# Splitting the second mixer's weights, and making its memory keys and values, during the first layer's way down

## The chip, the cores and the metric

The kernel runs on one core of a Trainium2 chip. The core has five engines with their own instruction queues: TensorE (PE in the profile, with its weight loads as PEld) multiplies matrices, VectorE (DVE), ScalarE (ACT) and GpSimd (POOL) work on rows of 128 partitions, and SyncE (SP) issues the transfers between DRAM and the on-chip buffer SBUF. PE writes its products into PSUM. Each engine has its own queue of instructions and waits on semaphores for the others. The metric is the time of one execution in microseconds, the median of several runs.

## The reference

A hybrid encoder trunk over 512 tokens of width 1024, in float32. `DEPTH` is 2, so there are two layers: layer 0 has a banded window mixer (A), layer 1 a global mixer (B). Cut to what matters:

```python
mem_n = rms_norm(mem, mem_norm_g)                  # 256 memory rows, the same for both layers
for i in range(DEPTH):
    h = rms_norm(x, g_mix_pre[i])
    proj = h @ w_in[i]                             # q (12 heads of 64), k, v (3 heads), qm (4 heads)
    ...
    tok = mixer(q, k, v)
    mkv = mem_n @ w_mem_kv[i]                      # memory keys and values, 4 heads
    mo = memory_attention(qm, km, vm)
    o = concatenate([tok, mo]) @ w_o[i]
    x = x + rms_norm(o, g_mix_post[i])
    h = rms_norm(x, g_ffn_pre[i])
    gu = h @ w_gate_up[i]
    f = (silu(gu[..., :D_FF]) * gu[..., D_FF:]) @ w_down[i]
    x = x + rms_norm(f, g_ffn_post[i])
```

The memory keys and values of layer 1 depend on the memory and on a weight only, not on anything that layer 0 computes.

## The kernel before

**Products of split numbers.** The operands of PE are typed fp32r. Each float32 operand is split into a high part (`hi`, the number copied to fp32r) and a low part (`lo`, the rest), and `mm3` (L218 to L222) makes a product out of three matmuls: hi by hi, hi by lo, lo by hi. A weight comes from DRAM in units of 128 x 1024 (512 KB; units of `wkv` are 128 x 768, 384 KB). `unit` (L185) loads a unit into a buffer `raw` (three of them), then `split` (L224) writes `hi` and `lo` into a ring of four slots each in the pool `whl`. The high part is made on ACT (L230) or POOL (L228), the low part on DVE (L234) or POOL (L232); a table of constants, `PACE`, says which for each unit of the mixers. A slot is free again when the last matmul that reads it is done. Other weights take slots of the same ring: the gate and up weights of the feed-forward part (`pair`, L891) and the units of `wd`.

**A mixer** (`mixer`, L622) lays its pieces of work on a time axis by constants of `PACE` (`put`), sorts them, and writes them out in that order; this is PE's order. The other engines' orders, SP's among them, are set when the kernel is compiled. In layer 1 the pieces are, by position: the keys and values of four token tiles (`kv_pieces`, with four units of `wkv`), the first group of queries (`q_pieces`, two units of `wq` for each of four groups), the memory keys and values in four pieces of two (`mem_pieces`, four units of `wm`; the first two lie behind the keys, the last two among the first queries), then sixteen heads of scores (`score`, L498; `score_mem`), transposes of the probabilities (`turn`, L569) and values (`value`, L583), with the queries of the next groups between them; at the end the first part of the output product (`heads_out`, four units of `wo`). The keys pass through a normalisation and a rotary embedding (`rope_b`, L388) on ACT, DVE and POOL, a split, and transposes on PE (`keys`, L365: L370 and L375, copied by ACT to `ka` and by DVE to `kb`).

**The memory rows.** The normalised memory, split and transposed, lies in `mT` (2 MB). Layer 0 makes it and stores it to DRAM (`spill`, L650); layer 1 loads it back in four transfers (L438).

**The feed-forward part** (`ffn`, L857) works in three lots of hidden columns (8, 6 and 8 tiles of 128; `LOTS`). In each lot `body` makes the hidden columns and `down` (L792) multiplies them by `wd` ("the way down"): for each half of the output and each unit of two tiles, 24 matmuls of 512 columns. Lots 0 and 1 have eight and six such steps. The third lot's way down is in `ffn_out` (L817), where the norms of the next layer's input follow token tile by token tile. Four units of `wd` for its second half are held at once.

Of the kernel before, what the change touches and what calls it, by code (L numbers as in the profile page):

```python
# [15 lines left out]
P = 128  # L16
# [4 lines left out]
DEPTH = 2  # L21
# [151 lines left out]
class Trunk:  # L173
    def __init__(self, tc, a):
        self.tc, self.nc, self.a = tc, tc.nc, a

    def pool(self, stack, name, side="left", **kw):
# [6 lines left out]

    def unit(self, src, side=0, pool=None, parts=1, put=None, x=0, dst=None, key=None):  # L185

        nc, n = self.nc, src.shape[-1]

        def load():
# [143 lines left out]
    def mem_pieces(self, l, mk, put, x0, dx, lag, xw):  # L333
# [23 lines left out]
        for u in range(4):  # L357
            for m in range(2):
                put(x0[u] + m * dx[u] / 2, lambda u=u, m=m: prod(u, m))

    def again(self, k2):

        self.nc.gpsimd.tensor_scalar(k2[:, :, P:], k2[:, :, :HD].bitcast(F32), 1.0, 1.0, op0=OP.mult, op1=OP.mult)
# [49 lines left out]
    def kv_pieces(self, l):  # L413
# [3 lines left out]
        self.vs = self.core.tile([P, NT, NG, P], F32R, name="vs", tag="vs")  # L417
        w = self.wkv if l == 0 else [self.unit(self.a["wkv"][l, u], side=self.side(l, "kw", u)) for u in range(4)]

        def prod(t, st, u):  # L420
# [8 lines left out]
            if u == 3:  # L429
                kv = ps[:, :384].rearrange("p (z h d) -> p z h d", z=2, d=HD)  # L430
                r = self.rs[:, t:t + 1]
                self.split_scaled(self.vs[:, t, :, :HD], self.vs[:, t, :, HD:], kv[:, 1], r)
                kx = self.core.tile([P, 4, HD], F32, tag="qx", name="kx", bufs=3)
                ins = nc.scalar.activation(kx[:, :NG], kv[:, 0], AF.Copy, scale=r).ins  # L434
                if l:
                    with self.tc.issue_after(ins):
                        z, ks = t // 2, slice(t % 2 * 4, t % 2 * 4 + 4)
                        nc.sync.dma_start(self.mT[:, z, ks].bitcast(F32), self.spill[:, z, ks])  # L438
                self.rope(l, kx, t, NG, 1)
                st["k2"] = self.core.tile([P, 4, 3 * HD], F32R, tag="q2", name="k2", bufs=3)  # L440
                self.split(st["k2"][:, :NG, :HD], st["k2"][:, :NG, HD:P], kx[:, :NG])
                self.again(st["k2"][:, :NG])
# [8 lines left out]
    def q_pieces(self, l, c, qTs, put, x0, lead):  # L451
        nc = self.nc
        w = {}
        for z in range(2):
            self.unit(self.a["wq"][l, c, z], self.side(l, "qw", 2 * c + z), put=put, x=x0 - lead + z * lead / 3, dst=w,
                      key=z)

# [164 lines left out]
    def mixer(self, l, mkp, late, tokp):  # L622
# [19 lines left out]
        def keys():  # L642
            for m in range(2):
# [84 lines left out]
    def heads_out(self, l, put, xw, xs, x0, dx):  # L728
# [3 lines left out]
        for u in range(4):  # L732
            self.unit(self.a["wo"][l, 0, u], self.side(l, "owm", u), put=put, x=xw + u / 4, dst=self.wo, key=u)

# [82 lines left out]
    def ffn_out(self, get, w, fs, o, head, gpost, gpre, resid, dst, rs):  # L817
# [16 lines left out]
        for u in range(nu):  # L834
            wu = head["w"] if u == 0 else self.unit(w[0, fs[0] // 2 + u])
            for t in range(0 if u else 2, NT):
                self.down_prod(ps[t], get, fs, u, t, wu)
        for t in range(NT):
            join(ps[t], t, 0)
# [17 lines left out]
    def ffn(self, l, pools, forms, late, done):  # L857
# [152 lines left out]
        pools["forms"].close()  # L1010

        for c, (f0, f1) in enumerate(LOTS):
            fs = list(range(f0, f1))
# [6 lines left out]
            p1(gs[0])  # L1020
            p2(gs[0])
            prep_b(gs[0])
            prep_d(gs[0])
# [58 lines left out]
    def run(self):  # L1082
        tc, nc, a = self.tc, self.nc, self.a
        with ExitStack() as top:
# [5 lines left out]
            self.ps, self.nbank = self.psum(top, "ps"), 0  # L1090
            dram = top.enter_context(tc.tile_pool(name="dram", bufs=1, space=bass.MemoryType.DRAM))
            xs = [[dram.tile([P, D], F32, name=f"x{i}{t}", tag=f"x{i}{t}") for t in range(NT)] for i in range(3)]
# [17 lines left out]
            for l in range(DEPTH):  # L1110
# [4 lines left out]
                mkp = self.pool(core, f"mk{l}")  # L1115
                self.mT = tokp.tile([P, 2, KD, NMEM], F32R, tag="tok", name="mT", bufs=1)
                if l == 0:
                    late = self.start(mkp)
                norm.close()
                self.core = self.pool(core, f"core{l}")  # L1120
# [54 lines left out]
```

## Time and profile before

| | |
|---|---|
| median of 3 runs | 1162.95 us (1162.56 to 1165.04) |
| the profiled execution | 1161.5 us, of which the span from first to last instruction is 1159.7 us |
| mean granted clock of TensorE | 0.988 |
| first mixer and its output | about 30 to 220 us |
| feed-forward part of layer 0 | about 220 to 570 us |
| second mixer | about 570 to 767 us |
| DMA traffic | 124.06 MB, mean 107 GB/s |

The page gives busy times of the engines; the views of the trace give single instructions with start, duration and what ended the engine's idle time before them. A matmul's duration is its way through the array; matmuls follow each other faster than that, so the distance of their starts is what they cost. The clock column of a table of windows is the share of full speed that TensorE was granted.

### The profile page before, as it was taken

Reading aid. Unit: us, or ns where it says so; the run is one execution under the profiler, and the core shown is the slowest. Engines: PE = TensorE matmul, PEld = TensorE weight load, DVE = VectorE, ACT = ScalarE, POOL = GpSimd, SP = SyncE. Lnnn points to the kernel's source line nnn. Section 1 sums busy time; section 2 is a strip of 40 time slices with the busy share of each in tenths; the row PEclk is TensorE's granted clock in tenths of the full one; section 3 lists DMA queues with packets and bytes.
Section 4 is the critical chain, followed back from the end, with each engine's and each line's share of the span. In section 5 each row is a group of like instructions: output and inputs, shape, how many; then the busy total and the mean of one; then the engine's idle time right before and its main releaser. Section 6 shows DMA issues by size and latency. Waiting matters only on the chain.

```text
span 1159.7 us, 19436 instructions
## 1 busy us (share of the span) xinstructions
PE 1106.9 (95%) x7448; PEld 1016.6 (88%) x7448; DVE 840.9 (73%) x1432; ACT 644.7 (56%) x1308; POOL 264.6 (23%) x394
## 2 busy tenths in 40 slices
PE   5999989999999999999898999799999999999997
PEld 4989878899989989998788888577999899899985
DVE  5678884798637866885778998846997458658854
ACT  5568783665425534653436888845665246436531
POOL 6445573200000000000454764433000000000001
PEclk9999999999999999999999999999999999999999
DMA  7521124533422342225523110234234323413243
GB/s 269 189 74 37 37 74 134 189 114 109 154 65 73 110 145 73 97 87 191 174 93 106 37 37 2 69 116 150 68 115 140 107 73 110 142 41 110 92 163 109
DMA packets 34316, 124.06 MB, mean 107 GB/s; under 512 B 3872, under 2 KB 4000, under 8 KB 34096
## 3 DMA queue, kind: packets, MB, share of 16 engines
q1 hardware_dynamic: 33984, 122.24, 32.0%
q8 instruction: 58, 0.95, 0.3%
q0 software_dynamic: 240, 0.60, 0.2%
q14 instruction: 34, 0.28, 0.1%
HBM read 112.33 MB, written 10.49 MB: 106 GB/s over the span
## 4 chain that ended last, share of the span: by engine, by line
PE 78%; DVE 9%; ACT 5%; POOL 3%; issue 3%; DMA 1%; SPq 0%; POOLq 0%; DVEq 0%; ACTq 0%
PE ps L220 12%; PE ps L221 12%; PE ps L222 12%; PE ps L930 11%; PE ps L932 11%; PE ps L931 11%; PE tp L576 2%; PE o L591 1%; PE o L590 1%; PE s L511 1%; DVE tl L234 1%; PE s L512 1%; DMA raw<-in_wkv_dram 1%; ACT whi L230 1%; ACT p L528 1%
## 5 line engine op out<-in xcount | busy, mean ns | idle before, releaser
L230 ACT ACTIVATE whi<-raw 128x1024 fp32r<-128x1024 f32 (+2 forms) x177 | 150.6, 860 | 208.6 <-PE ps L222 104.2
L234 DVE TENSOR_TENSOR wlo<-raw,whi 128x1024 fp32r<-128x1024 f32 (+2 forms) x171 | 171.5, 1009 | 89.9 <-ACT whi L230 74.2
L930 PE MATMUL ps<-sf,whi 128*128 128x256 f32 x640 | 180.3, 282 | 0.1
L932 PE MATMUL ps<-sf,whi 128*128 128x256 f32 x640 | 180.2, 282 | 0.0
L931 PE MATMUL ps<-sf,wlo 128*128 128x256 f32 x640 | 179.8, 281 | 0.0
L254 POOL TENSOR_SCALAR e<-sso 128x1 f32<-128x1 f32 x8 | 3.4, 423 | 634.7 <-ACT junk L249 634.6
L220 PE MATMUL ps<-whi,f 128*128 128x512 f32 x352 | 137.3, 390 | 0.0
L222 PE MATMUL ps<-whi,f 128*128 128x512 f32 x352 | 137.0, 389 | 0.0
L221 PE MATMUL ps<-wlo,f 128*128 128x512 f32 x352 | 137.0, 389 | 0.0
L930 PE MATMUL ps<-a,whi 128*128 128x256 f32 x480 | 134.5, 280 | 0.0
L932 PE MATMUL ps<-a,whi 128*128 128x256 f32 x480 | 134.0, 279 | 0.0
L931 PE MATMUL ps<-a,wlo 128*128 128x256 f32 x480 | 133.9, 279 | 0.0
L930 PEld LDWEIGHTS ps<-sf,whi 128*128 128x128 f32 x640 | 121.2, 189 | 1.1 <-ACT p L936 0.6
L931 PEld LDWEIGHTS ps<-sf,wlo 128*128 128x128 f32 x640 | 120.9, 189 | 0.5
L932 PEld LDWEIGHTS ps<-sf,whi 128*128 128x128 f32 x640 | 121.1, 189 | 0.0
L220 PE MATMUL ps<-whi,hT 128*128 128x256 f32 (+1 forms) x320 | 101.6, 318 | 1.8 <-ACT kx L434 1.8
L221 PE MATMUL ps<-wlo,hT 128*128 128x256 f32 (+1 forms) x320 | 96.8, 303 | 4.6 <-DVE wlo L234 3.4
L222 PE MATMUL ps<-whi,hT 128*128 128x256 f32 (+1 forms) x320 | 96.4, 301 | 0.8 <-DVE hT L234 0.8
L566 POOL TENSOR_SCALAR p<-p,rd 128x256 f32<-128x256 f32 (+2 forms) x128 | 74.9, 603 | 76.2 <-DVE rd L563 23.0
L930 PEld LDWEIGHTS ps<-a,whi 128*128 128x128 f32 x480 | 90.3, 188 | 0.2
L931 PEld LDWEIGHTS ps<-a,wlo 128*128 128x128 f32 x480 | 90.2, 188 | 0.2
L932 PEld LDWEIGHTS ps<-a,whi 128*128 128x128 f32 x480 | 90.2, 188 | 0.0
(202 smaller groups left out, 2805.0 us busy)
## 6 DMA issues: line engine op xcount, KB each, us to landing
raw<-in_wgu_dram SPq DMA_DIRECT2D x48, 512.0 KB, 4.3
raw<-in_wd_dram SPq DMA_DIRECT2D x44, 512.0 KB, 4.3
rb<-in_wgu_dram SPq DMA_DIRECT2D x40, 512.0 KB, 3.6
raw<-in_wq_dram SPq DMA_DIRECT2D x16, 512.0 KB, 3.8
raw<-in_wo_dram SPq DMA_DIRECT2D x16, 512.0 KB, 3.5
xt<-x SPq DMA_DIRECT2D x12, 512.0 KB, 4.1
raw<-in_wm_dram SPq DMA_DIRECT2D x8, 512.0 KB, 4.0
x<-y SPq DMA_DIRECT2D x8, 512.0 KB, 2.9
```

What stands on the lines that cost most here:

```text
L220: mm(out, lh, rh, start=first, stop=False)
L221: mm(out, lh, rl, start=False, stop=False)
L222: mm(out, ll, rh, start=False, stop=last)
L230: nc.scalar.activation(hi, src, AF.Copy)
L234: nc.vector.tensor_sub(lo, src, hi.bitcast(F32))
L511: nc.tensor.matmul(s[:, :n], qi, hd["ka"]()[:, k0 * P:k1 * P], start=True, stop=False)
L512: nc.tensor.matmul(s[:, :n], qi, hd["kb"]()[:, k0 * P:k1 * P], start=False, stop=True)
L566: self.pooled = nc.gpsimd.tensor_scalar(hd["p"][z][:, :n], hd["p"][z][:, :n], rd[:, z:z + 1], 1.0, op0=OP.mult, op1=OP.mult)
L576: nc.tensor.transpose(tp[:, z], hd["p"][i][:, jj * P:(jj + 1) * P], self.ident)
L930: mm(out, wh[:, s], rh, start=start and k == 0, stop=False, skip_group_check=True)
L931: mm(out, wl[:, s], rh, start=False, stop=False, skip_group_check=True)
L932: mm(out, wh[:, s], rl, start=False, stop=k == 3, skip_group_check=True)
```

## The change

`ahead` splits a unit of layer 1 in layer 0 and stores both halves in DRAM; `unit` with the new argument `pair` loads such halves straight into two slots of the ring, without `raw` and without a split. Sixteen units go this way: four of `wkv`, eight of `wq`, four of `wo` (the first half of its columns). One is done after each step of `down` in layer 0 (8 in lot 0, 6 in lot 1) and two in `ffn_out`.

`mem_ahead` loads `mT` from DRAM into a pool of its own after lot 0's `down`, takes the four units of `wm`, makes layer 1's memory keys and values for both tiles of 128 rows (48 matmuls), and leaves the transposes of the keys and the stores to DRAM for the place behind the first two products of lot 1. The mixer of layer 1 loads the result in three transfers (512 KB each); its `mem_pieces` and its four loads of `mT` are gone.

```diff
+    def ahead(self, name, *at):
+        nc, src = self.nc, self.a[name][at]
+        pair = self.unit(src)
+        n = src.shape[-1]
+        self.pairs[(name,) + at] = [self.dram.tile([P, n], F32, name="pair", tag="_".join(map(str, (name, z) + at)))
+                                    for z in range(2)]
+        for z in range(2):
+            nc.sync.dma_start(self.pairs[(name,) + at][z], pair[z][:, :n].bitcast(F32))
...
+        if pair in self.pairs:
+            def fetch():
+                t = [self.whl.tile([P, 1024], F32R, tag=z, name=f"w{z}", bufs=4) for z in ("hi", "lo")]
+                for z in range(2):
+                    nc.sync.dma_start(t[z][:, :n].bitcast(F32), self.pairs[pair][z])
+                return t
+
+            if put is None:
+                return fetch()
+            put(x, lambda: dst.__setitem__(key, fetch()))
+            return
...
+    def mem_ahead(self, l, pool):
+        nc = self.nc
+        mT = pool.tile([P, 2, KD, NMEM], F32R, tag="mT", name="mT", bufs=1)
+        nc.sync.dma_start(mT.bitcast(F32), self.spill)
+        mk = {z: pool.tile([P, NMH, NMEM], F32R, name=f"km{z}", tag=f"km{z}", bufs=1) for z in "ab"}
+        mk["v"] = pool.tile([P, 2, NMH, P], F32R, name="vm", tag="vm", bufs=1)
+        w = [self.unit(self.a["wm"][l, u]) for u in range(4)]
+        out = []
+        for m in range(2):
+            ps = self.tagged("s")
+            for k in range(KD):
+                ms = (slice(None), k, slice(m * P, (m + 1) * P))
+                c = slice((k % 2) * 512, (k % 2) * 512 + 512)
+                self.mm3(ps, mT[:, 0][ms], mT[:, 1][ms], w[k // 2][0][:, c], w[k // 2][1][:, c], k == 0, k == KD - 1)
...
+            out.append(lambda m=m, k2=k2: self.keys(k2, mk["a"], mk["b"], m, 4))
+
+        def store():
+            for z, t in mk.items():
+                self.kept[z] = self.dram.tile(list(t.shape), F32, name="kept", tag=f"kept{z}")
+                nc.sync.dma_start(self.kept[z], t.bitcast(F32))
+
+        return out + [store]
...
-        w = self.wkv if l == 0 else [self.unit(self.a["wkv"][l, u], side=self.side(l, "kw", u)) for u in range(4)]
+        w = self.wkv if l == 0 else [self.unit(self.a["wkv"][l, u], pair=("wkv", l, u)) for u in range(4)]
...
-                ins = nc.scalar.activation(kx[:, :NG], kv[:, 0], AF.Copy, scale=r).ins
-                if l:
-                    with self.tc.issue_after(ins):
-                        z, ks = t // 2, slice(t % 2 * 4, t % 2 * 4 + 4)
-                        nc.sync.dma_start(self.mT[:, z, ks].bitcast(F32), self.spill[:, z, ks])
+                nc.scalar.activation(kx[:, :NG], kv[:, 0], AF.Copy, scale=r)
...
+            for z, t in mk.items() if l else ():
+                nc.sync.dma_start(t.bitcast(F32), self.kept[z])
...
-        self.mem_pieces(l, mk, put, xm, [pc["m0dur"], pc["m0dur"], pc["mdur"], pc["mdur"]], pc["mlag"], xw)
+        if l == 0:
+            self.mem_pieces(l, mk, put, xm, [pc["m0dur"], pc["m0dur"], pc["mdur"], pc["mdur"]], pc["mlag"], xw)
...
+                if self.todo:
+                    self.ahead(*self.todo.pop(0))
...
+            for z in later:
+                z()
+            mst.close()
+            later = []
...
+                if l < DEPTH - 1 and c == 0:
+                    later = self.mem_ahead(l + 1, self.pool(mst, "mem", side="right"))
...
+                    self.todo = ([("wkv", 1, u) for u in range(4)] + [("wq", 1, c, u) for c in range(4) for u in range(2)]
+                                 + [("wo", 1, 0, u) for u in range(4)])
```

The queries and the output product pass `pair=("wq", l, c, z)` and `pair=("wo", l, 0, u)` to `unit` in the same way. The constants of `PACE` are the same before and after.

More of the change, by code (lines that the diff above doesn't have):

```diff
@@ L455, in q_pieces @@
             self.unit(self.a["wq"][l, c, z], self.side(l, "qw", 2 * c + z), put=put, x=x0 - lead + z * lead / 3, dst=w,
-                      key=z)
+                      key=z, pair=("wq", l, c, z))
         def prod(t, st, u):
@@ L642, in keys @@
         def keys():
-            for m in range(2):
+            for m in range(0 if l else 2):
                 self.ready(("m", m))
@@ L732, in heads_out @@
         for u in range(4):
-            self.unit(self.a["wo"][l, 0, u], self.side(l, "owm", u), put=put, x=xw + u / 4, dst=self.wo, key=u)
+            self.unit(self.a["wo"][l, 0, u], self.side(l, "owm", u), put=put, x=xw + u / 4, dst=self.wo, key=u,
+                      pair=("wo", l, 0, u))
         def part(k):
@@ L837, in ffn_out @@
                 self.down_prod(ps[t], get, fs, u, t, wu)
+            if self.todo:
+                self.ahead(*self.todo.pop(0))
         for t in range(NT):
@@ L1010, in ffn @@
         pools["forms"].close()
+        later, mst = [], ExitStack()
         for c, (f0, f1) in enumerate(LOTS):
@@ L1090, in run @@
             self.ps, self.nbank = self.psum(top, "ps"), 0
-            dram = top.enter_context(tc.tile_pool(name="dram", bufs=1, space=bass.MemoryType.DRAM))
+            dram = self.dram = top.enter_context(tc.tile_pool(name="dram", bufs=1, space=bass.MemoryType.DRAM))
+            self.kept = {}
             xs = [[dram.tile([P, D], F32, name=f"x{i}{t}", tag=f"x{i}{t}") for t in range(NT)] for i in range(3)]
```

11 lines of the change are left out of this document (9 added, 2 removed).

## The prediction

> **What bounds the kernel now.** The head of the page comes first: which engine is full.
>
> ```profile
> span 1159.7 us, 19436 instructions
> PE 1106.9 (95%) x7448; PEld 1016.6 (88%) x7448; DVE 840.9 (73%) x1432; ACT 644.7 (56%) x1308; POOL 264.6 (23%) x394
> ```
>
> TensorE (PE) is idle for only 1159.7 - 1106.9 = 52.8 us, so a change that leaves the matmuls as they are can win some part of that, plus time in which the clock was low. The next view is the table of windows, ten microseconds each, over the second mixer (about 570 to 767 us); these are its rows with the most idle PE. Columns: busy time of PE, weight load, DVE, ACT, POOL, then granted clock, DMA share, GB/s.
>
> ```profile
> 570.00:580.00 10.00, 6.60 (x31) 6.06 (x30) 7.86 (x11) 3.93 (x9) 5.89 (x8) 0.77 0.73 222
> ...
> 600.00:610.00 10.00, 6.84 (x51) 6.19 (x49) 8.51 (x18) 3.88 (x10) 5.29 (x8) 0.98 0.52 175
> ...
> 650.00:660.00 10.00, 8.95 (x61) 7.56 (x60) 9.96 (x21) 9.05 (x21) 9.35 (x12) 1.00 0.17 53
> ...
> 690.00:700.00 10.00, 8.44 (x59) 7.48 (x58) 8.62 (x20) 7.92 (x19) 6.67 (x9) 1.00 0.30 95
> ...
> 720.00:730.00 10.00, 7.28 (x46) 5.88 (x45) 9.98 (x17) 7.59 (x17) 8.93 (x9) 0.95 0.07 8
> 730.00:740.00 10.00, 7.64 (x42) 6.19 (x40) 7.59 (x16) 8.59 (x21) 4.27 (x7) 0.88 0.17 53
> 740.00:750.00 10.00, 8.72 (x59) 7.43 (x59) 7.70 (x15) 7.51 (x22) 4.72 (x9) 1.00 0.12 45
> 750.00:760.00 10.00, 8.81 (x52) 6.87 (x49) 7.74 (x15) 8.74 (x25) 4.44 (x10) 1.00 0.31 108
> ```
>
> Two early windows lose over 3 us each; the six later ones lose 1.05 + 1.56 + 2.72 + 2.36 + 1.28 + 1.19 = 10.2 us. The timeline of PE says what the early ones waited for. First the start of the keys and values (starts are in the first column, the releaser in the bracket):
>
> ```profile
> 569.42 0.39 PE L222 MATMUL ps<-whi,f 128*128 128x512 f32 x1
> ...
> 570.44 0.42 PE L220 MATMUL ps<-whi,hT 128*128 128x384 f32 x1
> ...
> 572.45 0.33 PE L222 MATMUL ps<-whi,hT 128*128 128x384 f32 x1
> 572.62 0.34 PE L220 MATMUL ps<-whi,hT 128*128 128x384 f32 x1
> 576.36 0.69 PE L221 MATMUL ps<-wlo,hT 128*128 128x384 f32 x1 [3.40 <-DVE wlo L234]
> 576.85 0.52 PE L222 MATMUL ps<-whi,hT 128*128 128x384 f32 x1
> ...
> 582.05 1.12 PE L297 MATMUL tp<-ident,h 128*128 128x128 f32 x8
> ```
>
> PE waits 3.4 us for the low half of a key/value weight, then runs slowly: 16 matmuls from 576.85 to 582.05 are 0.325 us apart, against 0.17 us before the wait. The second stall waits for a key copy (kb):
>
> ```profile
> 606.23 0.28 PE L221 MATMUL ps<-wlo,hT 128*128 128x256 f32 x1
> 606.35 0.28 PE L222 MATMUL ps<-whi,hT 128*128 128x256 f32 x1
> ...
> 610.09 0.59 PE L375 MATMUL tp<-identr,k 128*128 128x128 f32 x3 [3.25 <-DVE kb L376]
> 610.48 0.54 PE L220 MATMUL ps<-whi,hT 128*128 128x256 f32 x1
> ...
> 612.74 0.38 PE L221 MATMUL ps<-wlo,hT 128*128 128x256 f32 x1
> ```
>
> Again a wait, 3.25 us, then ten matmuls 0.226 us apart instead of 0.12.
>
> **Part 1: the memory keys move.** The first and last of twelve memory matmuls:
>
> ```profile
> 595.92 0.40 PE L220 MATMUL ps<-whi,mT 128*128 128x512 f32 x1
> ...
> 598.45 0.39 PE L222 MATMUL ps<-whi,mT 128*128 128x512 f32 x1
> ```
>
> 2.53 / 11 = 0.23 us each, and 2 x 8 x 3 = 48 of them: 11.0 us. They leave the mixer and are added behind lot 0 of the first layer, where PE has no gap, with their sixteen transposes. That is -11.0 and +11.0: **0**. The move alone wins nothing.
>
> **Part 2: the splits move.** What they cost in the mixer, from the groups by line and shape (566 to 767 us):
>
> ```profile
> L232 POOL TENSOR_TENSOR wlo<-raw,whi 128x512 fp32r<-128x512 f32 x16 | 22.4, 1409 | 0.0
> ...
> L234 DVE TENSOR_TENSOR wlo<-raw,whi 128x512 fp32r<-128x512 f32 x16 | 12.8, 822 | 1.4 <-ACT whi L230 0.8 <-POOL whi L228 0.5
> ...
> L230 ACT ACTIVATE whi<-raw 128x512 fp32r<-128x512 f32 x18 | 11.0, 635 | 2.9 <-PE ps L222 2.9
> ...
> L228 POOL TENSOR_SCALAR whi<-raw 128x512 fp32r<-128x512 f32 x14 | 9.9, 719 | 1.6 <-PE ps L222 1.5
> ...
> L234 DVE TENSOR_TENSOR wlo<-raw,whi 128x768 fp32r<-128x768 f32 x4 | 3.8, 951 | 0.0
> ...
> L230 ACT ACTIVATE whi<-raw 128x768 fp32r<-128x768 f32 x4 | 3.4, 838 | 0.6 <-PE ps L222 0.5
> ```
>
> The mixer loses 12.8 + 3.8 = 16.6 us of DVE, 14.4 us of ACT and 32.3 us of POOL. The same DVE multiply (L399), once beside an idle POOL and once while POOL was splitting weights:
>
> ```profile
> 589.77 0.36 DVE L399 TENSOR_TENSOR kx<-kx,r 128x192 f32<-128x192 f32 x1 [0.44 <-POOL r L245]
> ...
> 597.66 1.45 DVE L399 TENSOR_TENSOR kx<-kx,r 128x192 f32<-128x192 f32 x1 [0.15 <-POOL r L245]
> ```
>
> 0.36 against 1.45 us: with POOL's splits gone, DVE's chains shorten by more than its own 16.6 us. What PE gets of it:
>
> (a) The stall at 572. Each pair fetch needs a ring slot, free when the last tile of the way down has used it: units 0 to 3 about 565.5, 566.9, 568.2 and 569.6 (the last is the row 569.42; six matmuls, 1.36 us, lie between them). What a fetch takes:
>
> ```profile
> raw<-in_wq_dram SPq DMA_DIRECT2D x16, 512.0 KB, 3.8
> ...
> raw<-in_wkv_dram SPq DMA_DIRECT2D x8, 384.0 KB, 3.2
> ```
>
> ```profile
> 12.00:14.00 2.00, 1.17 (x4) 0.43 (x2) 0.75 (x2) 1.76 (x3) 1.49 (x1) 1.00 0.99 398
> ...
> 46.50:56.30 9.80, 9.80 (x84) 9.64 (x83) 5.40 (x16) 4.37 (x10) 3.39 (x3) 1.00 0.96 367
> ```
>
> The first of these windows is loads with every DMA engine busy, 398 GB/s; the second is a store to DRAM among loads, 367 GB/s. 384 KB (0.393 MB) is 1.0 us at such rates, so 3.2 - 1.0 = 2.2 us are latency. Eight halves end at 565.5 + 2.2 + 2.0 per unit: 569.7, 571.7, 573.7, 575.7. PE wants them from 570.44 on at 1.04 us a unit (six matmuls): it waits about 1.2 us for unit 2 and 1.0 us for unit 3. Gone are 3.4 + 16 x 0.155 = 5.9 us with the first slow matmul's part about 6.2; new are 2.2. **-4.0**, bounds 0 (the waits are as long as now) and -6.2.
>
> (b) The stall at 606. The copy was late because the rope of the last key tile stood behind weight splits and beside POOL; both go. 3.25 + 10 x 0.106 = 4.3 us; the chain behind the last tile stays. **-4.0**, bounds 0 and -4.3.
>
> (c) The 10.2 us in the six late windows. Weights of wo are split on POOL and DVE there, but so are the outputs of the heads, which stay. **-3.0**, bounds 0 and -8; nearer to nothing, since where DVE is fullest (650) PE loses only 1.05 us.
>
> (d) A new wait. The query weights took their turn in the raw buffers and needed only a split once a slot was free; memory matmuls covered it. Now their slot frees when the last key tile has used it, 18 x 0.17 = 3.1 us before the projection ends, and a pair of 512 KB takes 3.8 + 1.3 = 5.1 us, the next pair 2.6 us more. PE waits 2.0 us, works 12 x 0.12 = 1.4 us, waits 1.2 us. Behind these waits stand all later queries and scores in PE's order, and in SP's queue the next fetches. **+3.3**, bounds +1 (the queue runs ahead) and +8 (both go cold and other fetches come between).
>
> The rule of the Trainium skill, "TensorE: Matmul & The Clock Gate", Part 1, is that the clock halves after an idle window of about 3.4 us and returns after as long at work. The rows agree for 3.40 us; 3.25 us was enough too. By it waits of 2.0 and 1.2 us stay warm; were they to go cold, the sum would be about 2 us higher.
>
> **Part 3: the first layer's way down.** Its step, as ACT's rows show it, one split each step:
>
> ```profile
> 319.73 1.06 ACT L230 ACTIVATE whi<-raw 128x1024 fp32r<-128x1024 f32 x1 [4.38 <-PE ps L222]
> 325.17 1.06 ACT L230 ACTIVATE whi<-raw 128x1024 fp32r<-128x1024 f32 x1 [4.38 <-PE ps L222]
> ```
>
> ```profile
> 321.50:353.00 31.50, 31.50 (x145) 26.21 (x144) 11.85 (x14) 10.02 (x14) 0.00 (x0) 1.00 0.17 50
> ```
>
> A step is 5.44 us; ACT idles 4.38 us of it and DVE and ACT are busy a third: a second split (1.06 us ACT, about 1.2 us DVE) hides under PE. The DMAs do not hide so easily. A step with an added wq or wo unit moves four times 0.524 MB (two loads, two stores), 2.10 MB in 5.44 us: 385 GB/s, between the two rates above. At 367 GB/s it takes 5.71 us, 0.27 us too long, and there are 8 wq and 2 or more wo units: ten such steps, 2.7 us; at 398 GB/s nothing. In SP's queue a store waits for its split, and behind it stand the loads of the next units of wd, for which PE waits. The ring of four now holds two units of wd instead of four, so a load may be late by about 3 us (5.44 less a split of 2.3) before PE sees it. **+2.0** for both, bounds 0 and +11.6 (below).
>
> The Trainium skill, "DMA: Bandwidth & Descriptors", Specifications, gives about 358 GB/s as the limit of memory for one core. By that a step takes 5.86 us, ten of them lose 4.2 us, and the sum is 2.2 us higher; the row of 398 GB/s is above it, for two microseconds.
>
> The orders of SP, ACT, DVE and POOL are made anew at compile time, and the diff doesn't show them. SP's timeline now:
>
> ```profile
> 538.64 11.48 SPq L192 DMA_DIRECT2D raw<-in_wkv_dram  x3
> ```
>
> Three loads of wkv run some 20 to 30 us ahead of their use at 570, as soon as raw buffers are free; an order that lets transfers run ahead is likely again, so I take no loss for it, bounds -2 and +2.
>
> **Sum.** 0 - 4.0 - 4.0 - 3.0 + 3.3 + 2.0 = -5.7 us. The profiled execution took 1161.5 us (span 1159.7, 1.8 outside): 1155.8. The median of the runs is 1.45 above it: 1157.2, so I say **1157**.
>
> **Rivals.** A: the way down becomes bound by its transfers; this decides where the mixed rate falls below 385 GB/s for long. Lot 0 moves 4.2 MB of wd, 4.7 and 6.3 of added units, 2.1 of memory rows, 2.1 of wm and 1.6 of the next lot: 21.0 MB, 57.2 us at 367 GB/s, against 8 x 5.44 + 11.0 = 54.5. Lot 1 moves 3.1 + 9.4 + 1.6 = 14.1 MB, 38.4 us against 32.6. That is 2.7 + 5.8 = 8.5 us and about 3 us of low clock behind the two lots, 11.5 in place of 2.0: +3.8, 1167. For it speaks the 367 row, against it that the last stores block nobody. B: the waits change their name. Fetch waits replace split waits: (a) -1, (b) -4, (c) -2, (d) +5, way down +2, together 0: 1163. For it speaks that a fetch begins only when a slot is free. C: the relief of DVE and POOL reaches the heads: (a) -5, (b) -4, (c) -8, (d) +3.3, way down +1: -12.7, 1150. For it speaks DVE at 9.98 of 10 in two of the late windows; against it, that splits of tok and of the probabilities fill DVE there too and stay.
>
> **Chances.** Forecast 0.45 (its own range 1152 to 1161), A 0.25, B 0.18, C 0.12. Range 1149 to 1168. A measurement tells apart about 0.2%, 2.3 us: faster 0.56 (most of the forecast, C), same 0.18 (B, the forecast's edge), slower 0.26 (A, B's edge).
>
> **What would show it.** (a) No 3.4 us wait on wlo at the first keys, but waits on a DMA into whi or wlo of 1 to 2 us. (b) No wait on kb near the fourth key tile. (c) DVE's L399 near 0.36 us throughout. (d) PE waiting for a DMA at the first queries. Part 3: windows of the way down near 380 GB/s with PE still at full; PE waits on wlo or a DMA there mean A. The forecast is wrong if PE idles more than 4 us between the two mixers, or if the mixer isn't about 19 us shorter than now (11.0 and the 7.7 of (a) to (d)).

## The result: slower, and the profile after

The changed kernel takes 1170.61 us, the median of seven runs (1166.58 to 1172.31), beside 1162.95 us before (seven runs, 1161.85 to 1165.77): a ratio of 1.0058, 95% interval 1.0039 to 1.0076 (the ratio goes by all runs, so it can differ a little from that of the medians). That is 7.7 us slower where 5.7 us faster was forecast, and above the range. The profiled execution took 1170.55 us. The head of its page, busy time and share of the span for each engine:

```profile
span 1168.8 us, 19547 instructions
...
PE 1114.2 (95%) x7448; PEld 1018.8 (87%) x7448; DVE 838.3 (72%) x1432; ACT 652.7 (56%) x1306; POOL 231.1 (20%) x364
```

The number of matmuls is the same, 7448. PE is idle for 54.6 us instead of 52.8 and busy for 7.3 us more: the loss shows less as idle time than as matmuls that follow each other more slowly. To see where, cut PE's timeline at its landmarks and take the distances between starts of matmuls, in one profile of each kernel (us; the forecast's terms stand beside the stretch that each belongs to):

| stretch | before | after | difference | forecast |
|---|---|---|---|---|
| start to the first matmul of lot 0's way down | 304.27 | 303.67 | -0.6 | 0 |
| way down of lot 0 | 47.67 | 51.86 | +4.2 | |
| memory keys and values | 0 | 11.76 | +11.8 | |
| lot 1 up to its way down | 56.04 | 58.23 | +2.2 | |
| way down of lot 1 | 36.79 | 39.21 | +2.4 | |
| lot 2, its way down, to the first key matmul | 125.67 | 127.95 | +2.3 | these five: +11.0 +2.0 |
| keys and values of the second mixer | 25.31 | 29.21 | +3.9 | (a) -4.0 |
| from there to the first score | 33.64 | 21.03 | -12.6 | -11.0, (b) -4.0, (d) +3.3 |
| first score to the next layer's way down | 259.88 | 255.54 | -4.3 | (c) -3.0 |
| rest | 262.48 | 262.49 | 0.0 | 0 |

The differences add to +9.2 us, the span's +9.1. The last three terms came out within 1.4 us of the forecast. Two did not: the five stretches of the first layer cost 22.8 us instead of 13.0, and the keys lost 3.9 us instead of winning 4.0. (The start, whose work is untouched, lies anywhere from 301.8 to 305.8 us in the kernels below; differences of a us or two in one profile's total are not read. The stretch from the first score to the next way down is called the heads below. The expectations of the first four runs take the way down from a later landmark: 40.6 and 29.7 us before, 44.8 and 32.2 after.)

**The way down.** Windows of before (first fence) and after (second): busy PE, weight load, DVE, ACT, POOL, then granted clock, DMA share, GB/s.

```profile
320.00:340.00 20.00, 20.00 (x90) 16.57 (x89) 9.39 (x11) 6.25 (x8) 0.00 (x0) 1.00 0.28 81
```

```profile
303.67:355.53 51.86, 49.87 (x230) 41.20 (x229) 21.79 (x22) 22.21 (x27) 0.00 (x0) 0.97 0.87 303
...
320.00:340.00 20.00, 20.00 (x89) 16.54 (x89) 9.52 (x8) 9.53 (x12) 0.00 (x0) 1.00 0.93 341
340.00:356.00 16.00, 14.01 (x54) 10.83 (x53) 4.90 (x4) 5.97 (x8) 0.00 (x0) 0.89 0.83 279
...
440.00:460.00 20.00, 18.14 (x80) 14.48 (x79) 9.95 (x11) 6.60 (x7) 0.00 (x0) 1.00 0.87 320
```

In the same twenty microseconds the rate went from 81 to 341 GB/s, with the DMA engines at 0.93; over the whole way down of lot 0 (the first row of after) it is 303 at 0.87. DVE and ACT are still half empty, so their time isn't used up. PE holds out until the last steps of each lot and then idles for 1.99 us (lot 0) and 1.86 us (lot 1). What it waits for in lot 0, on PE's timeline, then ACT's:

```profile
347.52 0.51 PE L242 MATMUL ps<-whi,f 128*128 128x512 f32 x1 [1.24 <-ACT whi L252]
348.78 0.50 PE L243 MATMUL ps<-wlo,f 128*128 128x512 f32 x1 [0.75 <-DVE wlo L256]
```

```profile
346.41 1.06 ACT L252 ACTIVATE whi<-raw 128x1024 fp32r<-128x1024 f32 x1 [8.07 <-DMA raw<-in_wd_dram]
```

PE waits for ACT's split, and ACT had been idle for 8.07 us waiting for the load of a unit of `wd`. DVE's timeline shows when its raw buffer came free, and SP's where the load stood:

```profile
335.50 2.43 DVE L256 TENSOR_TENSOR wlo<-raw,whi 128x1024 fp32r<-128x1024 f32 x2 [2.50 <-ACT whi L252]
```

```profile
339.63 0.32 SPq L194 DMA_DIRECT2D pair<-wlo  x1
340.05 0.41 SPq L214 DMA_DIRECT2D raw<-in_wd_dram  x1
```

The raw buffers go round in turn, three of them, and the third load before this one was split by the first of the two DVE splits, which ends at 336.73. So the load could have gone out then; it stood behind the two stores of the last unit loaded before it, which waited for their splits, and was issued 3.3 us later, at 340.05. It then took 6.26 us to land, where the median of such loads before is 4.3. The last load of lot 1 has the same lateness, 3.3 us, and lands in 5.1. So there are two candidates: a slow rate, and an order of SP's queue that issues late.

**The keys.** They begin at 592.68 us. PE's timeline of the first token tile, then SP's:

```profile
594.79 0.44 PE L242 MATMUL ps<-whi,hT 128*128 128x384 f32 x1 [0.82 <-DMA whi<-pair]
596.40 0.69 PE L243 MATMUL ps<-wlo,hT 128*128 128x384 f32 x1 [1.17 <-DMA wlo<-pair]
596.88 0.52 PE L244 MATMUL ps<-whi,hT 128*128 128x384 f32 x1
597.21 0.52 PE L242 MATMUL ps<-whi,hT 128*128 128x384 f32 x1
...
602.49 0.69 PE L242 MATMUL ps<-whi,hT 128*128 128x384 f32 x1 [2.20 <-DMA whi<-pair]
603.45 0.69 PE L243 MATMUL ps<-wlo,hT 128*128 128x384 f32 x1 [0.27 <-DMA wlo<-pair]
```

```profile
590.20 0.32 SPq L768 DMA_DIRECT2D x<-o  x1
590.61 0.38 SPq L203 DMA_DIRECT2D whi<-pair  x1
...
596.47 0.32 SPq L768 DMA_DIRECT2D x<-o  x1
596.88 0.38 SPq L203 DMA_DIRECT2D whi<-pair  x1
```

The forecast's slot times, moved by the 22.24 us by which the mixer starts later, are 589.1 for the second unit and 591.8 for the fourth. The second is issued 1.5 us after its slot came free and the fourth 5.0 us after, each straight behind a store `x<-o`, which waits for its tile's norm. PE waits 4.46 us in all, and after the 1.17 us wait its matmuls are 0.32 us apart, not 0.17.

```profile
594.00:608.00 14.00, 9.57 (x29) 8.17 (x30) 3.99 (x6) 2.59 (x7) 3.20 (x8) 0.56 0.49 179
...
622.00:632.00 10.00, 7.39 (x61) 6.79 (x60) 6.72 (x21) 3.85 (x10) 3.18 (x6) 1.00 0.85 334
```

In the first row the clock is 0.56 of full for 14 us, though the idle pieces are short. The last row holds the wait (d), on PE's timeline:

```profile
623.45 0.36 PE L242 MATMUL ps<-whi,hT 128*128 128x256 f32 x1 [1.22 <-DMA whi<-pair]
...
626.15 0.39 PE L242 MATMUL ps<-whi,hT 128*128 128x256 f32 x1 [0.51 <-DMA whi<-pair]
627.41 0.39 PE L243 MATMUL ps<-wlo,hT 128*128 128x256 f32 x1 [0.88 <-DMA wlo<-pair]
```

2.6 us, against 3.3 forecast.

### The profile page after: what moved, and what is told of

It reads as the page before. It is cut to its first block, busy times and chain, and to the rows that moved or that the text cites. A ratio compares the mean times of both kernels' runs of the same rounds, so it can differ in the third digit from the quotient of the medians.

```text
span 1168.8 us, 19547 instructions
## 1 busy us (share of the span) xinstructions
PE 1114.2 (95%) x7448; PEld 1018.8 (87%) x7448; DVE 838.3 (72%) x1432; ACT 652.7 (56%) x1306; POOL 231.1 (20%) x364
## 4 chain that ended last, share of the span: by engine, by line
PE 73%; DMA 8%; DVE 7%; ACT 7%; issue 3%; POOL 2%; SPq 1%; ACTq 0%; DVEq 0%; POOLq 0%
PE ps L986 11%; PE ps L988 11%; PE ps L987 11%; PE ps L243 10%; PE ps L242 10%; PE ps L244 10%; PE tp L624 3%; ACT whi L252 2%; DMA raw<-in_wd_dram 2%; DMA raw<-in_wq_dram 2%; DVE wlo L256 2%; PE o L638 2%; PE o L639 2%; DMA raw<-in_wkv_dram 1%; PE s L559 1%
## 5 line engine op out<-in xcount | busy, mean ns | idle before, releaser
L252 ACT ACTIVATE whi<-raw 128x1024 fp32r<-128x1024 f32 (+2 forms) x175 | 156.3, 901 | 210.7 <-PE ps L988 79.9
L256 DVE TENSOR_TENSOR wlo<-raw,whi 128x1024 fp32r<-128x1024 f32 (+2 forms) x171 | 178.9, 1053 | 112.2 <-ACT whi L252 89.5
```

The lines of the kernel that those rows point to most:

```text
L252: nc.scalar.activation(hi, src, AF.Copy)
L256: nc.vector.tensor_sub(lo, src, hi.bitcast(F32))
```

## The experiments

The first theory was that there are two separate causes, bytes on the way down and the order of SP's queue at the keys. It has two rivals: the order of SP's queue is the cost of the way down too, or the weights' fetches are slow at the keys wherever they stand. Each ratio is against before, run beside it on the same chip.

**The two halves of the change.** First the memory part alone:

```diff
-                    self.todo = ([("wkv", 1, u) for u in range(4)] + [("wq", 1, c, u) for c in range(4) for u in range(2)]
-                                 + [("wo", 1, 0, u) for u in range(4)])
+                    self.todo = []
```

> Memory keys made in lot 0, no weights split ahead (all of wkv, wq, wo are split in the mixer as before). If the harm comes from the pairs alone, the way down of both lots keeps its 40.6 and 29.7 us, the feed-forward part grows by the 11.0 us of memory matmuls and 1 to 2 us, and the mixer loses 11 us and little else: 1161 to 1165 us. If moving the memory keys is itself harmful (its matmuls were cover in the mixer, or its 4 MB of loads starve the way down), the way down or the keys grow too: 1167 us or more.

1165.95 us, ratio 1.0024 [1.0012, 1.0037]: about 2.8 us slower. Both ways down are back at 47.67 and 36.79 us. The memory products take 11.19 us, as forecast, but lot 1 up to its way down takes 58.82 us instead of 56.04. PE's timeline at the start of lot 1, where the sixteen transposes of the memory keys stand:

```profile
366.42 0.46 PE L422 MATMUL tp<-identr,k 128*128 128x128 f32 x4
...
367.85 0.54 PE L422 MATMUL tp<-identr,k 128*128 128x128 f32 x4 [0.63 <-ACT kma L424]
368.79 0.51 PE L427 MATMUL tp<-identr,k 128*128 128x128 f32 x4 [0.39 <-DVE kmb L428]
369.13 0.35 PE L986 MATMUL ps<-sf,whi 128*128 128x256 f32 x1
```

They take 369.13 - 366.42 = 2.7 us, since the second half needs the buffers that ACT and DVE are still copying. And the mixer wins only 9.7 us from the keys to the first score: PE now waits there for the keys' own chain (1.20 us for `kx`, 1.61 for `k`), beside which the memory products stood before. So part 1 isn't 0 but a loss of some 3 us.

Then the weights alone, with `mem_ahead` taken out and `mem_pieces` and the loads of `mT` put back as before:

```diff
-                if l < DEPTH - 1 and c == 0:
-                    later = self.mem_ahead(l + 1, self.pool(mst, "mem", side="right"))
...
-        if l == 0:
+        if True:
             self.mem_pieces(l, mk, put, xm, [pc["m0dur"], pc["m0dur"], pc["mdur"], pc["mdur"]], pc["mlag"], xw)
```

> Weights split ahead, memory keys in the mixer as before. If the pairs are the harm, the way down of lots 0 and 1 grows by about 6 us as in the changed kernel, the keys by 4 us, and the mixer wins back 4 to 8 us elsewhere, with memory matmuls covering the wait for the first queries: 1163 to 1168 us. If memory keys were the harm: 1157 us or less.

1166.62 us, ratio 1.0036 [1.0017, 1.0055]. The ways down take 50.08 and 42.87 us: 2.4 and 6.1 us lost without any memory rows. Keys 27.23 (before 25.31), first score to the next way down 253.88: 6.0 us won. From the keys to the first score it takes 35.63 us, 2.0 lost. The two ratios add to 1.0060, close to the change's 1.0058, but not stretch by stretch: the way down of lot 1 loses 6.1 us here and 2.4 in the change, whose lot 1 moves the same units.

**What holds up the way down.** Splits and loads stay, but only the first unit of each width is stored, and all fetches read that one, so fourteen of the sixteen units are not the reference's weights in layer 1:

```diff
+        if n in self.kept:
+            self.pairs[(name,) + at] = self.kept[n]
+            return
+        self.kept[n] = self.pairs[(name,) + at] = [...]
```

> The changed kernel, but only the halves of the first wkv unit and of the first wq unit are stored, and all fetches read these (same bytes in the mixer, weights not the reference's). Loads and splits of all sixteen units stay. If stores (as bytes or as an order) make the way down late, its lots take 40.6 to 41.5 and 29.7 to 30.5 us: about 1162 us. If the ring and the raw buffers shared with the added units do it, the lots stay at 44.8 and 32.2 us: 1169 us.

The ways down are exactly as before, 47.67 and 36.79 us: the splits on ACT and DVE and the added loads cost nothing there. The total, 1165.29 us (1.0012 [0.9997, 1.0027]), wins less than that, because the memory part takes 16.62 us instead of 11.76. PE's timeline there, and DVE's:

```profile
361.55 0.79 PE L246 MATMUL ps<-wlo,mT 128*128 128x512 f32 x1 [3.71 <-DVE wlo L259]
```

```profile
358.94 0.69 DVE L967 TENSOR_TENSOR ru<-raw,rb 128x512 f32<-128x512 f32 x1 [3.07 <-DMA raw<-in_wgu_dram]
...
360.28 1.22 DVE L259 TENSOR_TENSOR wlo<-raw,whi 128x1024 fp32r<-128x1024 f32 x1
```

The order of DVE's queue, made anew, has work of lot 1 that waits 3.07 us for a load ahead of the last low half of `wm`. That is a loss of this order: in the change the last two low halves of `wm` (357.98) stand ahead of the first such work (360.30).

Are the stores too many bytes, or do they stand in the way in SP's queue? They are moved to GpSimd's queue, then to ACT's:

```diff
-            nc.sync.dma_start(self.pairs[(name,) + at][z], pair[z][:, :n].bitcast(F32))
+            nc.gpsimd.dma_start(self.pairs[(name,) + at][z], pair[z][:, :n].bitcast(F32))
```

> The changed kernel with the stores of the halves issued from GpSimd's queue, which is idle there, instead of SyncE's; same bytes. If loads of wd are late because they stand behind stores that wait for their splits (order in SyncE's queue), the way down returns from 44.8 and 32.2 us to about 41 and 30 us: 1164 us. If the bytes are the limit, both lots stay as they are: 1170 us.

1189.96 us, ratio 1.0223 [1.0191, 1.0255]. The way down of lot 0 takes 53.35 us, the memory part 21.26 and lot 2 up to its way down 88.49 (before 76.08). DMA groups of after, then of this run, median us from issue to landing last:

```profile
pair<-whi SPq DMA_DIRECT2D x12, 512.0 KB, 3.5
pair<-wlo SPq DMA_DIRECT2D x12, 512.0 KB, 4.0
```

```profile
pair<-whi POOLq DMA_DIRECT2D x12, 512.0 KB, 5.9
pair<-wlo POOLq DMA_DIRECT2D x12, 512.0 KB, 6.8
```

The stores land 2.4 and 2.8 us later, and hold the ring's slots that much longer: by the view of the tile `pair`, ACT's splits wait 40.8 us for them, in 12 waits, where it was 11.2 us in 3. The orders of the other queues changed as well, so this run says nothing clean of SP's. The same stores from ACT's queue:

> The changed kernel with the stores of the halves issued from ScalarE's queue instead of SyncE's; same bytes. If wd's loads are late because they stand behind stores in SyncE's queue, lots 0 and 1 of the way down return from 51.9 and 39.2 to 47.7 to 48.5 and 36.8 to 37.5 us (before: 47.7 and 36.8), total 1163 us. If the bytes are the limit, they stay within 1 us: 1170 us.

1180.94 us, ratio 1.0164 [1.0138, 1.0191]. The ways down take 51.08 and 38.45 us, hardly less than after. (Lost besides are the memory part, 20.68, and lot 2 up to its way down, 84.26 us.) No store stands in SP's queue ahead of the loads any more, and yet this doesn't clear the order of the queues: it moved to ACT's. A store of DVE's half stands there ahead of ACT's next work, and PE waits for that. ACT's timeline in lot 0, then PE's:

```profile
333.99 0.60 ACT L858 ACTIVATE o<-ps 128x512 f32<-128x512 f32 x1 [3.61 <-DVE wlo L256]
```

```profile
334.64 0.50 PE L242 MATMUL ps<-whi,f 128*128 128x512 f32 x1 [0.81 <-ACT o L858]
```

The other two waits of PE in this way down (0.33 and 0.43 us) are for splits that ACT began late in the same way. The stores also land later than from SP's queue, after 6.6 and 7.5 us. Then the bytes alone: only half of each half is stored, the fetch reads it twice, and the weights fetched are again not the reference's:

```diff
-            nc.sync.dma_start(self.pairs[(name,) + at][z], pair[z][:, :n].bitcast(F32))
+            nc.sync.dma_start(self.pairs[(name,) + at][z], pair[z][:, :n // 2].bitcast(F32))
```

> The changed kernel with stores of only the first half of each hi and lo (half the store bytes, the same waits and the same order in SyncE's queue); the mixer fetches that half twice, so the weights are not the reference's. If the bytes are the limit (1.57 instead of 2.10 MB a step, 289 GB/s), the way down takes 47.7 to 48.5 and 36.8 to 37.5 us: about 1164 us. If the order is, it stays at 51 and 39 us.

As many stores, with 1.57 MB a step in place of 2.10: the ways down are at 47.66 and 36.78 us. The whole way down of lot 0:

```profile
305.81:353.48 47.67, 47.67 (x230) 40.14 (x229) 22.61 (x23) 21.96 (x27) 0.00 (x0) 1.00 0.82 269
```

PE is full to the end, at 269 GB/s where it was 303. But the order of SP's queue isn't the change's either. The last load of `wd` of lot 0 now stands ahead of the stores of the unit loaded just before it:

```profile
334.46 0.48 SPq L215 DMA_DIRECT2D raw<-in_wd_dram  x1
339.85 0.32 SPq L194 DMA_DIRECT2D pair<-whi  x1
```

It goes out 0.4 us after its buffer came free, where it was 3.3 in the change, and it lands in 6.04 us, hardly faster than the change's 6.26. Lot 1 has the same 0.4 against 3.3, with a landing in 3.9 against 5.1. So this run has fewer bytes and a better order at once. **What is shown is that the stores cost the ways down their 6.6 us** (few stores: nothing lost). Whether they do so by their bytes or by standing ahead of loads isn't separated by these runs; in lot 0 the traces lean to the order. The total, 1172.56 us (1.0088 [1.0062, 1.0114]), doesn't profit: the memory part takes 15.68 us and lot 2 up to its way down 79.43 us, with PE waiting on DVE again.

**The keys.** The four fetches of `wkv` are issued before the last store of x:

```diff
+        if self.hold is not None:
+            with self.tc.issue_after(self.hold):
+                nc.sync.dma_start(dst[t], y)
...
+            if gn is not None and t == NT - 1:
+                self.wkv = [self.unit(self.a["wkv"][1, u], pair=("wkv", 1, u)) for u in range(4)]
+                self.hold = self.fins
```

> The changed kernel with one swap in SyncE's queue: the fetch of the last wkv unit stands before the store of the last token tile of x, not behind it. If the keys are late because that fetch waits in the queue for the norm (store at 596.5, slot free at 591.4), the keys' stretch falls from 29.2 to about 25 us and the total by 4 us: 1166 us. If the fetches are late by their bytes, the last unit lands no earlier than 2 us before: 1169 us or more.

1164.8 us, ratio 1.0032 [1.0013, 1.0051]; the keys take 23.92 us instead of 29.21. SP's timeline of this run:

```profile
594.32 0.38 SPq L203 DMA_DIRECT2D whi<-pair  x1
...
597.90 0.32 SPq L769 DMA_DIRECT2D x<-o  x1
```

The fourth fetch goes out 0.8 us after its slot's time (591.8 + 1.7 = 593.5 in this run) and 3.6 us ahead of the store. So the order was the cause; 1.4 us are left of the 4.0 that (a) promised against before. The size is less certain than one pair of profiles says: over all kernels that fetch `wkv` this way, the keys take 27.2 to 29.3 us with the store ahead and 23.9 to 26.4 with the fetch ahead, and the ratios of this run and of the change lie about 3 us apart.

> The changed kernel without the wkv units in the list: they are loaded into the raw buffers and split in the mixer as before. The keys return from 29.2 to 25.3 us. The way down of lot 0 now carries eight wq and wo units of 2.1 MB a step (four of them were 1.7 MB): by bytes it grows from 51.9 to 53 us or more; lot 1 has four steps with an added unit instead of six, and falls from 39.2 to about 38. Total 1166 us.

Twelve units, without `wkv`: 1167.42 us, ratio 1.0041 [1.0025, 1.0057]. Keys 26.55 us with the split wait of before, and the way down of lot 0, which now has eight units of 512 KB in place of four of 384 and four of 512, takes 55.55 us instead of 51.86. That fits the bytes, and the order as well: the last load of `wd` stands behind four stores here too, and goes out about 5.5 us after its buffer came free. The way down of lot 1, with four units instead of six, takes 37.31 us.

**Fewer stores, spread out.** Whether it is bytes or order, steps without an added unit should help. Three kernels, each with the same counter in both loops:

```diff
-                if self.todo:
+                self.step += 1
+                if self.todo and self.step % SKIP != SKIP - 1:
                     self.ahead(*self.todo.pop(0))
```

The first two have `SKIP = 3` and twelve units (`wkv` 4, `wq` of groups 1 to 3, two of `wo`) with the fetches ahead of the store, without and with the memory part; the third has `SKIP = 2`, no memory part and nine units (`wq` of groups 1 to 3, three of `wo`).

> The weights without the memory part: the memory keys and values stay in the second mixer, with their loads of the memory rows. Twelve units are split ahead (four of wkv, six of wq for the later queries, two of wo), after two of every three steps of the way down instead of after each, and the last wkv fetch stands ahead of the last store of x. If bytes per step are the limit of the way down: over three steps 3 x 1.05 MB of what the step moves anyway less the pairs, that is about two thirds of the added 1.57 MB per step, near 290 GB/s; lot 0's way down 47.7 to 48.5 us (before 47.67, all steps 50.1 to 53), lot 1's 36.8 to 37.5. If the order in SP's queue was the cost at the keys: keys near 24 us (before 25.3, the change 29.2). Heads about 254 to 255 (before 259.9). In all 1156 to 1160. Rival, the loss only moves to another engine's order, as in the runs with few stores and with half the bytes (2.7 to 4 us behind a way down): 1163 or more.

1162.47 us, ratio 0.9992 [0.9976, 1.0007]. The ways down are at 47.67 and 36.78 us, the keys at 24.65. But it takes 37.77 us from the keys to the first score (before 33.64), and the heads win only 2.9. The wait on the key copy is still there. DVE's timeline ahead of it, and PE's:

```profile
606.24 1.09 DVE L257 TENSOR_TENSOR wlo<-raw,whi 128x512 fp32r<-128x512 f32 x1
...
609.44 0.55 DVE L429 CAST kb<-tp 128x384 fp32r<-128x384 f32 x1
```

```profile
610.14 0.60 PE L428 MATMUL tp<-identr,k 128*128 128x128 f32 x3 [3.25 <-DVE kb L429]
```

`wkv` is split ahead here; the halves that DVE makes among the rope (606.24) are 512 columns wide, those of `wm` and the first `wq` units. The wait on kb of 3.2 us stands in every kernel that splits both of these in the mixer (before, this one and the two below without the memory part). It is 0.2 us or none in the kernels where one of the two is gone, among them the memory part alone (where PE waits 1.61 us for `k` instead) and the weights alone.

> The whole change with the same two edits: the memory keys made ahead, twelve units split ahead after two of every three steps, the last wkv fetch ahead of the last store of x. If both causes are met: way down of lot 0 47.7 to 49, memory part 11.2 to 12, lot 1 58.2 to 58.8 (its transposes of the memory keys cost 2 to 3), lot 1's way down 36.8 to 37.5, keys near 24, from the keys to the first score about 21, heads 254 to 255: 1157 to 1161. Rival, the loss moves to the memory part or to lot 2 by a new order on DVE or ACT (memory part 15 to 16, lot 2 near 79): 1163 to 1166. Against the run without the memory part it should be slower by the 2 to 3 us of the transposes, less what the shorter mixer gains at the first queries.

1164.47 us, ratio 1.0014 [1.0001, 1.0027]: by the ratios 5 us better than the change, still not faster than before. The ways down are clean (47.67, 36.79 us), but the keys take 26.40 us instead of the 24 expected, the memory part 13.75 us with a wait on DVE as in the run with few stores (2.30 us), lot 1 up to its way down 59.38, and the heads win only 2.3 us.

> Only nine units are split ahead, six of wq for the later queries and three of wo, after every second step; wkv, the first queries' weights and the memory keys stay as before. Way down 47.67 and 36.79 as before, keys 25.3, keys to first score 33.6, and the heads win what all runs with pairs have won, 4 to 5 us of 259.9: 1158 to 1160. If the heads' gain came from wkv or the memory part being gone, the heads stay at 258 to 260 and the time within 1 us of before, 1162 to 1164.

**1159.13 us, ratio 0.9967 [0.9954, 0.9980]**: faster than before. Ways down 47.67 and 36.79, keys 25.41, heads 252.61 us: 7.3 us won. From the keys to the first score 37.31 us, 3.7 us lost. PE's timeline there:

```profile
625.98 0.36 PE L243 MATMUL ps<-whi,hT 128*128 128x256 f32 x1 [1.99 <-DMA whi<-pair]
```

That is the first fetch of a second-group weight, which SP issues only at about 621 us. The last kernel splits that group in the mixer again and takes the fourth `wo` unit instead, eight units in all:

```diff
-[("wq", 1, c, u) for c in range(1, 4) for u in range(2)] + [("wo", 1, 0, u) for u in range(3)]
+[("wq", 1, c, u) for c in range(2, 4) for u in range(2)] + [("wo", 1, 0, u) for u in range(4)]
```

> As the run with nine units after every second step, but with the second group's two wq units split in the mixer again and the fourth wo unit split ahead: eight units, four of wq for the third and fourth groups and four of wo. In the run before, PE waited 1.99 us for the fetch of the second group's first unit (before: no wait there) and the stretch from the keys to the first score took 37.3 us against 33.6. If that fetch, which can only begin when a slot is free, is what it cost: the stretch is back at 33.6 to 34.5, the heads keep 253 to 255 of 259.9, and the time is 1156 to 1158. Rival, the fetch was covered and the stretch is long for another reason (the orders remade, the boundary of the first score moved into it): the stretch stays near 37 or the heads give back what it gains, 1159 to 1161.

**1154.75 us, ratio 0.9936 [0.9916, 0.9955]**, better than both kernels and 1.3 us below what was expected. From the keys to the first score 34.91 us, heads 253.88 us: 6.0 us won and 1.3 us lost. Its way down:

```profile
320.00:340.00 20.00, 20.00 (x90) 16.53 (x90) 11.06 (x12) 9.00 (x11) 0.00 (x0) 1.00 0.82 283
340.00:352.00 12.00, 12.00 (x57) 10.05 (x56) 4.88 (x7) 4.41 (x6) 0.00 (x0) 1.00 0.08 31
```

283 GB/s with PE full, and DMA engines that are nearly idle in the last 12 us, where the change still waited for its last loads of `wd`.

## Why the prediction was wrong

**Part 3, +2.0, is the step that failed most.** It was to cover what the first layer loses beside the 11.0 us of memory products; that came to 22.8 - 11.0 = 11.8 us, of which about 2.2 are the transposes of part 1. Two parts of the step failed. It priced bytes by the deficit of ten steps at 367 GB/s, and left the memory rows, `wm` and the next lot's loads out of that sum, though rival A had counted them. And it named the right wait ("in SP's queue a store waits for its split, and behind it stand the loads") but took the 3 us by which a load may be late as enough. The last load of lot 0 was 3.3 us late in the queue and about 2 us more in landing. The stores are shown as the cause (without them both ways down are as before); how much of it is bytes and how much order stays open, since no run changed one and kept the other.

**Rival A came out in its total, partly by luck.** Its price was 11.5 us. At the 341 GB/s of the 320 to 340 window its 21.0 MB take 61.6 us (measured 51.86 + 11.76 = 63.6) and its 14.1 MB 41.3 us (measured 39.21). But the trace moves only 17.9 MB in those 63.6 us, 282 GB/s. A also set its bytes against 8 x 5.44 + 11.0 = 54.5 us, where the way down of before and the memory products take 47.67 + 11.19 = 58.9; at its own 367 GB/s lot 0 would have cost nothing. The windows came to 341 GB/s instead of the 380 that was to be seen.

The Trainium skill, "DMA: Bandwidth & Descriptors", Specifications, gives about 358 GB/s for one core. The window's 341 lies below it; the 398 of the loads before does not. The forecast's 4.2 us by this rule, in place of 2.0, were too little as well.

**(a), -4.0, had the wrong sign.** The split wait went, and the times at which slots come free were right. What the step missed is that the fetches share SP's queue with the stores of x. Part 3 asked that question for the way down ("a store waits for its split, and behind it stand the loads"), and for the queues' new orders the forecast took "no loss". The run with the fetches ahead has 5.3 us less in the keys, about two thirds of the 7.9 us by which (a) was off; the rest are fetch waits and the clock.

**Part 1, 0**, was short by some 3 us (ratio 1.0024 alone): transposes without cover (2.7 us), and, as far as the traces show, memory products that had covered the keys' chain.

**(b) and (d) came out**: no wait on kb, 2.6 us of fetch waits for 3.3, and together with part 1 the stretch won 12.6 for 11.7. Which splits cause (b) was left loose; the runs point to those of `wm` and the first `wq` together, not to those of `wkv`.

**(c), -3.0, was right in size and bigger than it looked**: 4.3 us here; 5.9 to 7.3 with the weights alone, with the fetches first, without `wkv` and in the last two kernels, which all split three or four `wo` units ahead; 4.4 to 5.9 in the four runs on the stores; 2.3 and 2.9 in the two with only two `wo` units; and 1.8 us lost with none. `wkv` and the memory part aren't needed for it; that it is the `wo` units wasn't tried apart. DVE's multiply takes 0.35 to 0.36 us at all four key tiles of after, as forecast.

What was said to stay, the splits of the probabilities, does stay: in the fastest kernel PE still has this wait on its timeline, 2.74 us before.

```profile
733.40 0.66 PE L629 MATMUL tp<-ident,p 128*128 128x128 f32 x4 [2.73 <-DVE tl L257]
```

Both conditions that were named for a wrong forecast were met: PE's waits of over 0.1 us between the two mixers add to 5.8 us (3.85 of them at the ends of the two ways down), and the mixer is 13.0 us shorter (from its first key matmul to the first of its output product, 185.4 and 172.4), not 19. Rival B was right for the keys, where a wait changed its name and grew; C's gain did not reach the heads in the change itself.

Open: which choice of the order-making puts lot 1's work ahead of the last half of `wm` on DVE (3.7 us with few stores, 2.3 us in the spread version) wasn't tried apart. So whether the memory part can be made to pay isn't settled.

## What to carry to other kernels

Work moved into a stretch where the engines are idle must also fit its transfers, by their bytes and by the order of the queue that issues them. Add up everything that the stretch moves, prefetches for what follows included, and compare it with the rate that a trace reaches there, not with the best rate seen: here 265 and 269 GB/s over the whole way down of lot 0 left PE full, and 298 to 308 did not, though there the queue's order was part of it. Then look for loads that stand behind stores which wait. Move only the part that a late stage is short of (here eight units, of `wq` for the last two groups and of `wo`), at every second step, and leave what has a cheap place already. A transfer without a condition, behind one that waits for a result in the same queue, inherits its wait.

## What the hardware showed that was not expected

**Short waits halve the clock.** In after, idle pieces of 0.82 and 1.17 us within 2.5 us were followed by matmuls 0.32 us apart, and a clock of 0.56 over 14 us. Before has it too, after one wait of 1.72 us and with a delay of two us, on PE's timeline:

```profile
635.10 0.50 PE L511 MATMUL s<-ka,qT 128*128 128x512 f32 x1 [1.72 <-ACT p L528]
635.43 0.39 PE L512 MATMUL s<-kb,qT 128*128 128x512 f32 x1
...
637.25 0.63 PE L511 MATMUL s<-ka,qT 128*128 128x512 f32 x1
637.68 0.63 PE L512 MATMUL s<-kb,qT 128*128 128x512 f32 x1
```

The same pair of matmuls goes from 0.33 to 0.43 us apart. Yet 1.22, 0.51 and 0.88 us at the first queries of after left the clock at 1.00. The Trainium skill, "TensorE: Matmul & The Clock Gate", Part 1, has an idle window of about 3.4 us halve the clock; these rows went by shorter ones. How the pieces lie counts, and the clock records of the fourteen traces show part of it. The half clock comes in whole pieces of 3.41 us (in after 349.88 to 353.30 and 595.64 to 609.29), and within a trace all its starts between 100 and 1100 us lie whole multiples of 3.41 us apart, so the pieces lie on a fixed grid. Ahead of every start PE had idled 1.33 us or more in the one piece before it (1.45 us ahead of 595.64); with more than 1.81 us the drop always came, and in between it came in some cases only. The three waits at the first queries fall into three pieces of the grid, with at most 1.02 us idle in one.

**A full DMA share has no fixed rate.** Two windows of after, both with PE full and 12 us apart, show it:

```profile
328.00:332.00 4.00, 4.00 (x19) 3.34 (x18) 0.23 (x1) 1.32 (x2) 0.00 (x0) 1.00 0.96 353
340.00:344.00 4.00, 4.00 (x19) 3.33 (x18) 0.00 (x0) 0.00 (x0) 0.00 (x0) 1.00 1.06 311
```

Before, loads alone reached 398 GB/s at a share of 0.99; here, with stores among them, 353 at 0.96 and 311 at 1.06.
